# Reordering the stages of a fused decoder block on eight cores: start-up, attention projections, output buffers, and the passage from mixer to MLP

## The chip, the cores and the metric

One Trainium2 chip, eight cores, one program on all of them. Each core handles one half sequence (4096 tokens) of four sequences of 8192, with a halo of earlier tokens that it recomputes. The time is device microseconds (us) of the slowest core. Executions come in two states. In the slow one the cores of a die, or of both, show a lower granted TensorE clock and the time is some per cent longer, whatever the kernel. Engines: PE is TensorE (PEld its weight loads), DVE is VectorE, ACT is ScalarE, POOL is GpSimd, SP is SyncE, which issues the plain transfers; POOL issues the transfers that cast f32 weights to bf16.

## The reference, cut to what matters

```python
h = rms_norm(x, norm_mix_g)
a_b, a_c, a_v, q, k, v, g_a, g_b = split(h @ w_in)          # 1024 -> 5888 columns
y_a = (a_b * causal_dwconv(a_c * a_v)) @ w_proj_a           # gated convolution
# attention: 12 heads of 64 in 3 groups, window/dilation (128,1), (512,4), (2048,16)
y_b = merge_by_denominator(dilated_window_attention(q, k, v)) @ w_proj_b
x = x + (sigmoid(g_a + b0) * y_a + sigmoid(g_b + b1) * y_b) @ w_out
h = rms_norm(x, norm_ffn_g)
gate, val = split(causal_dwconv(h @ w_up))                  # 2 x 2816 columns
x = x + (silu(gate) * val) @ w_down
return rms_norm(x, final_norm_g)
```

## The kernel before

The kernel has three phases. A *tick* is one call of the hook that the program puts between groups of matmuls: it emits the next step of the norm, of a U block or of an attention item. A norms x (written as bf16 to a buffer `h_d` in memory), projects V, K and Q, and runs the attention items; an item is two score matmuls, an exponential on ACT, a mask multiply, and four value matmuls, and every second item sends an unnormalised output U (128 x 264 f32) to memory. B reads h and U back: convolution branch, merging of U, gates, output projection. C is the MLP. All phases share one on-chip arena, so a buffer's place is also an order: a new tenant waits for the old one.

A helper records every operation, with the keys that it reads and writes, and derives the waits. The program is therefore told here by the order of such calls. The start: one semaphore for all small constants, tile -1 (halo) first, and a loop that norms each block from end to end on VectorE.

```python
cdma(flagt_f := sb("flagf", [128, 16], F32), flag_d[:, :], "flagf")
emit_xload(); emit_xload()
wload(wK01, wcols(2304, 512), ("wK01",))
cdma(g1b, g1_d.partition_broadcast(128), ("g1b",))
...                                       # V, K2, V2, masks, Q, Q2, five small constants
for o_ in cops:
    o_.ev = cops[-1].ev                   # every constant waits for the last one
...                                       # memsets of Qz01, Qz2, QhZ on VectorE

def norm_front(...):                      # statistics and multiply in one go
    norm_mul(..., norm_stat(xap, xkey, hbap, hbkey, n))

SEQ = [-1, 0, -2, 1, "E", -3, 2, -4, 3, 4, 5, 6, 7]
for _ in range(10):
    tick(force=True)                      # the first blocks before any matmul
```

The attention items: two in flight, three output buffers, the masks of the third group all on POOL.

```python
LAG = 2
def mask_eng(st):
    return "pool" if st["g"] == 2 else "dve"
...
    if c == 1:
        ui = un[0] % 3                    # UA: 3 output buffers
        copy(pick(430, 400), UA[ui], ps[b][:, 0:4 * VW], ...)
        S.add("sp", lambda e: e.dma_start(out=dst, in_=UA[ui]), ...)
```

The end of A: the third group's V2, K2 and Q2 of tiles 4 to 7 in a pass of their own that reads h back, then the strided V, then B's weights and the last 32 items.

```python
        if t < 4:
            ...                           # V2, K2, Q2 of tiles 0..3 inside the tile
hs_load(0); hs_load(1)                    # tiles 4..7 of h from h_d
...
for jj in range(4):
    ...                                   # v_2, k_2, q_2 on hS
while att or att2 or pend:
    att_tick()
v2_load(2)
wload(wPB, ...); wload(wPA, ...); wload(wO, ...)
push_g2(2)                                # the last 32 items
hb_load(0)
while att or att2 or pend:
    att_tick()
...
for _ in range(3):
    ub_load()                             # only now the first U blocks
```

The passage from B to C: everything of the second norm after B's last output projection.

```python
        else:                             # last tile of B
            for p in (6, 7, 8, 9, 10):
                wu_load(p)                # ten half weights, issued by POOL
            wout(j)
for p in range(3):
    wd_load(p)
...
xn_load(); xn_load()
for _ in range(1 + len(BB[0])):
    c_stat(); c_mul(); c_back()
```

The softmax here doesn't subtract the row's maximum and nothing guards it: scores larger than these inputs give would overflow.

Of the kernel before, what the change touches and what calls it, by code (L numbers as in the profile page):

```python
# [128 lines left out]
def build_program():  # L129
# [129 lines left out]
    def cdma(dst, src, key):  # L259
        cops.append(S.add("sp", lambda e: e.dma_start(out=dst, in_=src), writes=[key], dma_sem=sem_c))  # L260
# [8 lines left out]
    hTA = [buf("hTA%d" % i, (W + 43520 + i * 8192) if i < 2 else R1 + 16384, [128, KC, 512], BF16) for i in range(3)]  # L269
# [8 lines left out]
    UA = [buf("UA%d" % i, R3 + 41344 + i * 1056, [128, 4 * VW], F32) for i in range(3)]  # L278
    V1s = [buf("V1s_%d" % i, R5 + i * 2112, [128, 4, 4, VW], BF16) for i in range(3)]
    K2 = [buf("K2_%d" % i, R4 + i * 8192, [128, 2, 16, 128], BF16) for i in range(2)]  # L280
    Qz2 = buf("Qz2", R4 + 16384, [128, 2, 16, 2, 128], BF16)
    V2 = [buf("V2_%d" % i, W + 8192 + i * 8448, [128, 16, 4, VW], BF16) for i in range(2)]
# [8 lines left out]
    sem_ht = [newsem("s_ht%d" % i) for i in range(3)]  # L291
# [4 lines left out]
    sem_u = [newsem("s_u%d" % i) for i in range(3)]  # L296
# [30 lines left out]
    SEQ = [-1, 0, -2, 1, "E", -3, 2, -4, 3, 4, 5, 6, 7]  # L327
# [3 lines left out]
    for t in SEQ:  # L331
        if t == "E":
            continue
        s_ = k % 3
        k += 1
        slot_of[t] = s_
        prev_in_slot[t] = last.get(s_)
        last[s_] = t
# [23 lines left out]
    cdma(flagt_f := sb("flagf", [128, 16], F32), flag_d[:, :], "flagf")  # L362
# [3 lines left out]
    cdma(g1b, g1_d.partition_broadcast(128), ("g1b",))  # L366
    gdma(ident, cmat_d[:, 0:128], "ident")
    emit_xload()
    emit_xload()
    wload(wV01, wcols(3072, 512), ("wV01",))  # L370
    wload(wK2, wcols(2816, 256), ("wK2",))
    wload(wV2, wcols(3584, 256), ("wV2",))
    gdma(mask4, cmat_d[:, 128:640], "mask4")
    gdma(hmask, cmat_d[:, 640:704], "hmask")
    wload(wQ01, wcols(1536, 512), ("wQ01",))
    wload(wQ2, wcols(2048, 256), ("wQ2",))
    cdma(bg, bg_d[:, :], "bg")
    cdma(caw, caw_d[:, :], "caw")
    cdma(cab, cab_d[:, :], "cab")
    cdma(fcw, fcw_d[:, :], "fcw")  # L380
    cdma(fcb, fcb_d[:, :], "fcb")
    for o_ in cops:
        o_.ev = cops[-1].ev
    for o_ in gops:
        o_.ev = gops[-1].ev
    S.add("dve", lambda e: e.tensor_copy(out=flagt, in_=flagt_f), reads=["flagf"], writes=["flagt"])
    S.add("dve", lambda e: e.memset(onest, 1.0), writes=["onest"])
    scale_g(g1b, ("g1b",))
    for i in range(2):
        S.add("dve", lambda e, i=i: e.memset(Qz01[i].rearrange("p a b c d -> p (a b c d)"), 0.0),  # L390
              writes=[("Qz01_%d" % i, c, h) for c in range(4) for h in range(2)])
    S.add("dve", lambda e: e.memset(Qz2.rearrange("p a b c d -> p (a b c d)"), 0.0),
          writes=[("Qz2", c, jj, h) for c in range(2) for jj in range(4) for h in range(2)])
    S.add("dve", lambda e: e.memset(QhZ.rearrange("p a b c -> p (a b c)"), 0.0), writes=["QhZ"])
# [32 lines left out]
    nf, nt = [0], [0]  # L427
    front_tick = {}
    tickno = [0]

    def can_front(i):
        t, b = NBL[i]
        return t == "E" or prev_in_slot[t] is None or prev_in_slot[t] in done_tiles

    def front(i):
        t, b = NBL[i]
        n = 16 if t == "E" else 128
        norm_front(xA[i % 4], ("xA%d" % (i % 4),), hbA[i % 2], ("hbA%d" % (i % 2),), n, g1b, ("g1b",))
        emit_xload()
        front_tick[i] = tickno[0]  # L440
# [17 lines left out]
    def norm_tick(force=False):  # L458
        if nt[0] < nf[0] and (force or tickno[0] - front_tick[nt[0]] >= 2):
            back(nt[0])  # L460
            nt[0] += 1
        if nf[0] < len(NBL) and nf[0] - nt[0] < 2 and can_front(nf[0]):
            front(nf[0])
            nf[0] += 1
# [10 lines left out]
    LAG = 2  # L475

    def mask_eng(st):
        return "pool" if st["g"] == 2 else "dve"

    def stage_a(st):  # L480
        k_ = att_n[0]
        att_n[0] += 1
        sbk = 4 + k_ % 2
# [15 lines left out]

    ob = [0]  # L500
    un = [0]

    def stage_b(st):
# [12 lines left out]
        if c == 1:  # L516
            ui = un[0] % 3
# [74 lines left out]
    def push_g2(s):  # L592
        cur, prv = s % 2, (s + 1) % 2
        rows = u_d[4 + 2048 * (s - 1):4 + 2048 * s, 2, :].rearrange("(i r) c -> r i c", r=16)
        for r in range(16):
            for c in range(2):
# [6 lines left out]
                                ck=[("K2", cur, s), ("K2", prv, s - 1), ("Q2", 0, s)],  # L603
# [1034 lines left out]
```

## Time and profile before

| | |
|---|---|
| median of the first 3 executions | 2384.74 us (2379.39 to 2619.54) |
| TensorE busy, profiled core (2393.8 us) | 85% |
| first B convolution, mean of 8 cores | 682.7 us |
| from there to the first up-projection | 739.3 us |
| from there to the end | 947.8 us |

B's first convolution and C's first up-projection are both the first matmuls with 388 columns after a gap, because the first tile of both phases is 388 wide. These three stages, as means over the cores of one fast profiled execution, add up to the mean span. The lines of the profile that carry the argument stand in the prediction. One more of before is from the table of waits in B from 735 to 1379.5 us, without its first 35 us (engine, line and tile that waited, for whom; us in total, times, longest us), where L1058 is the transposition of a normalised U block and L1044 the multiply that makes it:

```profile
PE ps L1058 <- DVE arena L1044: 17.2, 19, 1.8
```

TensorE meets 19 U blocks whose multiply is not done yet, for about 0.9 us each. In B's first 35 us (700 to 735) there are four more such waits, 12.0 us.

### The profile page before, as it was taken

What the parts mean: (1) busy time and instruction counts of PE and PEld (TensorE: products, weight loads), DVE (VectorE), ACT (ScalarE), POOL (GpSimd) and SP (SyncE); (2) the same over time, 40 slices, a digit from 0 to 9 for tenths busy, and PEclk for the clock granted to TensorE, in tenths of its full rate; (3) what the DMA queues carried; (4) which work ended last, traced back from release to release, by engine and by line L of the source; (5) the groups of instructions that cost most, each with busy time, mean ns of one, the idle gap of its engine ahead of it and who ended that gap; (6) DMA issues with size and microseconds to landing.
All of it is one profiled execution on the core that took longest, in us unless ns stands there. A gap on an engine that the chain in (4) does not pass through costs nothing.

```text
span 2393.8 us, 38186 instructions; the slowest of 8 cores (2354.9 to 2393.8 us)
## 1 busy us (share of the span) xinstructions
PE 2043.7 (85%) x11550; PEld 1049.2 (44%) x11550; DVE 1270.1 (53%) x2171; ACT 856.3 (36%) x1791; POOL 622.3 (26%) x1216
## 2 busy tenths in 40 slices
PE   0578767794658999999999928999999999999998
PEld 0344444452425555444444414555554444444443
DVE  4455554551224444443443316677677676858583
ACT  1243334441322222212111205455455453636362
POOL 1000000230141211111001223454454444434342
PEclk9999889997859999999999968999999999999999
DMA  9544356239651623330221597201201112111101
GB/s 154 113 111 99 100 117 146 62 80 174 123 138 62 129 87 98 98 115 25 92 95 36 88 164 145 80 26 65 71 28 62 63 45 71 45 72 36 62 19 44
DMA packets 128319, 205.88 MB, mean 86 GB/s; under 512 B 9684, under 2 KB 90330, under 8 KB 127736
## 3 DMA queue, kind: packets, MB, share of 16 engines
q1 hardware_dynamic: 86072, 169.19, 24.9%
q0 software_dynamic: 42048, 34.26, 10.7%
q8 instruction: 98, 1.61, 0.3%
q14 instruction: 101, 0.83, 0.1%
HBM read 177.05 MB, written 60.63 MB: 99 GB/s over the span
## 4 chain that ended last, share of the span: by engine, by line
PE 68%; DVE 10%; issue 9%; DMA 7%; POOL 3%; ACT 2%; SPq 1%; DVEq 1%; POOLq 0%; ACTq 0%
PE ps L608 47%; PE ps L1409 12%; PE ps L614 3%; PE ps L1204 3%; DMA u_d<-arena 3%; DMA arena<-h_d 2%; DVE arena L1358 2%; PE ps L420 2%; DVE arena L409 1%; DVE rtmp L319 1%; POOL arena L495 1%; PE ps L488 1%; DMA fcb_s<-fcb 1%; DVE rstd L321 1%; PE ps L512 1%
## 5 line engine op out<-in xcount | busy, mean ns | idle before, releaser
L608 PE MATMUL ps<-arena 128*128 128x512 bf16 (+5 forms) x6848 | 1352.3, 359 | 2.7 <-DVE arena L424 2.0
L608 PEld LDWEIGHTS ps<-arena 128*128 128x128 bf16 x6848 | 664.2, 98 | 655.9 <-issue 19.2
L1358 DVE SCALAR_TENSOR_TENSOR arena<-ps,fcw_s,arena 128x511 f32<-128x511 f32 (+4 forms) x792 | 524.9, 687 | 108.2 <-ACT uc L1349 30.3
L1409 PE MATMUL ps<-arena 128*128 128x512 bf16 x1408 | 311.3, 379 | 5.0 <-POOL arena L1362 2.8
L1351 ACT ACTIVATE arena<-ps,fcb_s,fcw_s 128x512 f32<-128x512 f32 (+1 forms) x396 | 284.3, 730 | 0.0
L401 ACT ACTIVATE arena<-arena 128x1024 bf16<-128x1024 f32 (+1 forms) x114 | 120.0, 1053 | 351.9 <-DVE arena L1415 205.1
L1371 POOL TENSOR_TENSOR arena<-arena 128x512 bf16<-128x512 bf16 (+1 forms) x198 | 210.5, 1063 | 97.9 <-ACT uc L1349 60.4
L1172 DVE TENSOR_TENSOR arena<-ps,arena 128x512 f32<-128x512 f32 (+2 forms) x144 | 91.0, 633 | 251.7 <-PE ps L608 245.6
L1409 PEld LDWEIGHTS ps<-arena 128*128 128x128 bf16 x1408 | 136.2, 98 | 167.3 <-issue 10.3
L420 PE MATMUL ps<-ident,arena 128*128 128x128 bf16 (+2 forms) x656 | 58.0, 240 | 152.5 <-DVE arena L409 147.5
L1158 ACT ACTIVATE arena<-ps,bg_s 128x512 f32<-128x512 f32 (+2 forms) x144 | 92.1, 640 | 252.4 <-PE ps L608 252.4
L252 ACT ACTIVATE arena<-ps 128x512 bf16<-128x512 f32 (+4 forms) x152 | 82.7, 544 | 219.9 <-PE ps L608 126.5
L1369 ACT ACTIVATE arena<-arena 128x512 bf16<-128x512 f32 (+1 forms) x198 | 115.2, 582 | 114.6 <-POOL arena L1362 97.6
L614 PE MATMUL ps<-arena 128*128 128x256 bf16 (+2 forms) x688 | 125.6, 340 | 35.8 <-DMA arena<-h_d 34.5
L491 ACT ACTIVATE arena<-ps 128x512 bf16<-128x512 f32 x192 | 109.7, 595 | 123.2 <-PE ps L488 62.9
L1175 POOL TENSOR_TENSOR arena<-arena 128x512 bf16<-128x512 f32 (+2 forms) x72 | 82.6, 1148 | 264.0 <-DVE arena L1172 238.0
L495 POOL TENSOR_TENSOR arena<-arena,mask 128x512 bf16<-128x512 bf16 x64 | 72.0, 1151 | 284.2 <-ACT arena L491 284.1
L512 PE MATMUL ps<-arena 128*128 128x66 bf16 x768 | 60.0, 206 | 97.7 <-DVE arena L495 48.9
L1362 POOL TENSOR_TENSOR arena<-arena,corr 128x2 f32<-128x2 f32 x352 | 84.2, 242 | 203.2 <-DVE arena L1358 192.3
L409 DVE SCALAR_TENSOR_TENSOR arena<-arena,rstd 128x1024 bf16<-128x1024 f32 (+1 forms) x82 | 105.3, 1285 | 58.7 <-POOL rstd L321 51.3
L420 PEld LDWEIGHTS ps<-ident,arena 128*128 128x128 bf16 (+2 forms) x656 | 47.9, 109 | 174.8 <-issue 165.4
L1204 PE MATMUL ps<-arena 128*128 128x512 bf16 (+1 forms) x528 | 120.2, 383 | 2.5 <-POOL arena L1175 2.5
(88 smaller groups left out, 1223.5 us busy)
## 6 DMA issues: line engine op xcount, KB each, us to landing
arena<-x_loc SPq DMA_DIRECT2D x80, 512.0 KB, 4.8
arena<-x_d SPq DMA_DIRECT2D x64, 512.0 KB, 3.6
x_d<-arena SPq DMA_DIRECT2D x32, 512.0 KB, 4.0
out<-arena SPq DMA_DIRECT2D x32, 512.0 KB, 2.6
u_d<-arena SPq DMA_DIRECT2D x96, 132.0 KB, 3.5
arena<-u_d SPq DMA_DIRECT2D x32, 396.0 KB, 3.3
arena<-w_up POOLq DMA_DIRECT2D x22, 512.0 KB, 18.5
arena<-w_in POOLq DMA_DIRECT2D x10, 1024.0 KB, 28.0
```

Of the source, the lines that this page charges most:

```text
L401: S.add("act", lambda e: e.activation(out=junk[0:n, :], in_=xap[0:n, :], func=AF.Square, accum_out=ssq[0:n, col:col + 1]), reads=[xkey] + ...
L409: S.add("dve", lambda e: e.scalar_tensor_tensor(out=hbap[0:n, :], in0=xap[0:n, :], scalar=rstd[0:n, col:col + 1], in1=gb[0:n, :], op0=ALU. ...
L420: S.add("pe", lambda e, kc=kc: e.transpose(out=psb[t][:, kc * 128:kc * 128 + n], in_=hbap[0:n, kc * 128:(kc + 1) * 128], identity=ident[0: ...
L491: S.add("act", lambda e: e.activation(out=PA[pi], in_=ps[sbk], func=AF.Exp, scale=0.125), reads=[("ps", sbk)], writes=[("PA%d" % pi,)])
L608: S.add("pe", lambda e, kc=kc: e.matmul(out, lhsT=wap[:, kc, col0:col0 + 128], rhs=rhs(kc), start=(kc == 0), stop=(kc == kcn - 1), skip_gr ...
L614: S.add("pe", lambda e, kc=kc: e.matmul(out, lhsT=lhs(kc), rhs=wap[:, kc, c0:c0 + n], start=(kc == 0), stop=(kc == KC - 1), skip_group_che ...
L1204: S.add("pe", lambda e, b=b, kc=kc, hf=hf: e.matmul(ps[b][0:n, :], lhsT=mT[:, kc, c0:c0 + n], rhs=wO[:, kc, hf * 512:(hf + 1) * 512], star ...
L1351: S.add("act", lambda e, b=b, t=t, ch=ch, w2_=w2_: e.activation(out=tmpC[t][:, 0:n], in_=ps[b][:, o:w_], func=AF.Identity, scale=w2_, bias ...
L1358: S.add("dve", lambda e, b=b, t=t, sh=sh, wv_=wv_, lo=lo: e.scalar_tensor_tensor(out=tmpC[t][:, lo:n], in0=ps[b][:, o + lo - sh:w_ - sh], ...
L1369: S.add("act", lambda e: e.activation(out=actT[:, p, 0:n], in_=tmpC[tg][:, 0:n], func=AF.Silu), reads=[("tmpC%d" % tg,)], writes=[("actT", ...
L1371: S.add("pool", lambda e: e.tensor_tensor(out=actT[:, p, 0:n], in0=actT[:, p, 0:n], in1=tmpC[tv][:, 0:n], op=ALU.mult), reads=[("tmpC%d" % ...
L1409: S.add("pe", lambda e, b=banks[hf], k_=k_, kk=kk, wt=wt, hf=hf: e.matmul(ps[b], lhsT=actT[:, k_, bi * 128:(bi + 1) * 128], rhs=wt[:, kk, ...
```

## The change

Its intent: keep TensorE fed where it idles. (1) x and V's weight first, tile 0 before tile -1, own semaphores, norm split into three steps that overlap. (2) Four h buffers on chip, V2, K2 and Q2 inside every tile, no reload. (3) Seven output buffers, four items in flight, half of the third group's masks and (from block 8 on) the small norm operations moved between engines. (4) B's first U blocks before the last items have ended, and U blocks paced. (5) C's first norm under B's last tile. Also in the diff: six on-chip banks for scores in place of two for the last 32 items (the *drain* of A, below), memsets moved from VectorE to ScalarE and POOL, and the convolution and gate weights loaded before A's projections have ended. Cut to its core:

```diff
-    SEQ = [-1, 0, -2, 1, "E", -3, 2, -4, 3, 4, 5, 6, 7]
+    SEQ = [0, -1, -2, 1, "E", -3, 2, -4, 3, 4, 5, 6, 7]
-    cdma(flagt_f := sb("flagf", [128, 16], F32), flag_d[:, :], "flagf")
+    emit_xload()
+    cdma(g1b, g1_d.partition_broadcast(128), ("g1b",), newsem("s_g1b"))
+    emit_xload()
+    wload(ident, cmat_d[:, 0:128], "ident")
+    wload(wV01, wcols(3072, 512), ("wV01",))
 ...
+        cols_a[i] = norm_stat(xA[i % 4], ..., n, "dve" if i < 8 else "pool")
 ...                                     # stat, mul and back are separate steps of a tick
-    LAG = 2
+    LAG = 4
-        return "pool" if st["g"] == 2 else "dve"
+        return "pool" if st["g"] == 2 and st["r"] % 2 else "dve"
-            ui = un[0] % 3
+            ui = un[0] % 7
 ...
-        if t < 4:
+        (V2, K2, Q2 in every tile)
-    hs_load(0)
-    hs_load(1)
-    (pass over tiles 4..7)
 ...
     hb_load(0)
-    while att or att2 or pend:
-        att_tick()
     for _ in range(3):
         ub_load()
+    while att or att2 or pend:
+        att_tick()
+        if ub_f[0] < 2 and len(att2) < 16 - 8 * ub_f[0]:
+            ub_front()
+    hb_load(1)
+    wload(wO, ...)
 ...
-        if (… ub_f[0] - ub_b[0] < 2 and ub_list[ub_f[0]][0] - 2 <= b_done[0]):
+        if (… and (force or ub_list[i][0] == 0 or tickno[0] - max(ub_ltick[i], ub_tick.get(i - 1, 0)) >= 6)):
             ub_front()
 ...
         if j == 8:
             for p in (3, 4, 5):
                 wu_load(p)
+            begin_c()                    # x1, gain row, statistics and multiply of two blocks
 ...
         else:
+            mid_c()                      # their transposes, and two more blocks
             for p in (6, 7, 8, 9, 10):
                 wu_load(p)
             wout(j)
-    for p in range(3):
-        wd_load(p)                       # now at pairs 4, 8 and 12 of C's first tile (a pair: 128 gate and 128 value columns)
```

## The prediction

> **What bounds the kernel now.** I read the page first: busy shares, slices, then the chain that ended last.
>
> ```profile
> PE 2043.7 (85%) x11550; PEld 1049.2 (44%) x11550; DVE 1270.1 (53%) x2171; ACT 856.3 (36%) x1791; POOL 622.3 (26%) x1216
> ...
> PE   0578767794658999999999928999999999999998
> ...
> PEclk9999889997859999999999968999999999999999
> DMA  9544356239651623330221597201201112111101
> ```
>
> TensorE is busy 85% of the span and no other engine comes near, so I look for its idle time: 2393.8 - 2043.7 = 350 us. A slice is 59.8 us. The idle lies in the first 13 slices (0 to 778 us, one of them full) and in the 24th; the rest is 90% or nearly so. I then cut the span where the program changes stage and asked for busy time and clock in each stretch (start:end, length, busy PE, PEld, DVE, ACT, POOL with counts, granted clock, DMA share, GB/s).
>
> ```profile
> 0.00:98.00 98.00, 16.70 (x118) 11.71 (x119) 49.39 (x100) 16.94 (x29) 9.80 (x31) 1.00 0.82 142
> 98.00:155.00 57.00, 49.56 (x380) 28.57 (x379) 22.44 (x52) 20.77 (x38) 0.59 (x3) 1.00 0.45 103
> 155.00:540.00 385.00, 297.65 (x2176) 168.46 (x2176) 209.04 (x486) 162.57 (x314) 38.31 (x35) 0.91 0.46 102
> 540.00:700.00 160.00, 81.78 (x577) 46.43 (x576) 30.08 (x61) 40.82 (x72) 42.60 (x42) 0.70 0.75 138
> 700.00:735.00 35.00, 22.99 (x129) 12.75 (x130) 17.76 (x45) 3.77 (x7) 0.39 (x2) 0.75 0.61 177
> 735.00:1379.50 644.50, 624.82 (x3275) 311.86 (x3273) 270.13 (x468) 136.96 (x211) 99.84 (x119) 1.00 0.31 82
> 1379.50:1395.50 16.00, 15.66 (x64) 6.56 (x64) 5.06 (x8) 0.00 (x0) 5.89 (x7) 0.89 0.95 147
> 1395.50:1446.60 51.10, 3.38 (x32) 2.64 (x33) 7.85 (x9) 5.54 (x9) 13.71 (x30) 0.55 1.13 182
> ```
>
> Idle: 81 us before the first full tile at 98, 95 in 98:540 (attention, "phase A"), 78 in 540:700, 12 in 700:735, 48 in 1395:1446 (the passage from the mixer, B, to the MLP, C). That is 314 of the 350; B and C are TensorE-bound and stay. What each waits for, from the chain in order of time (start, us, what):
>
> ```profile
> 6.70 18.60 DMA fcb_s<-fcb
> ...
> 402.75 12.36 DMA u_d<-arena
> ...
> 457.41 13.36 DMA u_d<-arena
> ...
> 548.41 46.29 DMA arena<-h_d
> ...
> 635.03 15.41 DMA arena<-v_d
> 652.37 23.90 DMA u_d<-arena
> ...
> 709.89 11.29 DMA arena<-u_d
> ```
>
> The start waits for the last small constant (one shared semaphore), then for 16 us of memsets on VectorE and eight norm blocks in series at 5.07 us each. The waits of 12, 13 and 24 us are score outputs that cannot leave their three buffers. The 46 us is tiles 4 to 7 of h read back from memory, the 15 us the strided V that has just been written. In 98:540 the table of waits puts most of TensorE's idle at a score mask on VectorE (48.1 us, 23 times) and the norm multiply (20.7 us).
>
> **What the Trainium skill says.** "TensorE: Matmul & The Clock Gate", Part 1, gives N/2.4 GHz + 2.5 ns start to start warm, half the rate after an idle window. The trace agrees: eight 512-column matmuls take 1.73 us (0.216 each) in the busy stretches, and the granted clock falls to 0.70 and 0.55 in the idle ones. So removed idle also speeds the work beside it. "DMA: Bandwidth & Descriptors", "Issuing engines are not separate DMA queues", says that transfers of all engines interleave on the same 16 engines. The trace agrees: in the first 60 us the casting weight loads (4.90 MB, 64.3%) and the plain loads (4.31 MB, 29.0%) together fill 93%. The weights move 4.90 / (0.643 x 60) = 127 GB/s of what they write, the plain loads 248. "GPSIMD Engine Reference", section 3.1, has two-input elementwise work slower there than on VectorE; here a mask takes 1151 ns on POOL against 456 ns on VectorE.
>
> **The change, part by part.** I need A's TensorE work at the warm rate, from counts in the source. 1112 matmuls of 512 columns x 0.216 = 240 us; 408 of 256 columns x 0.109 = 44; 192 attention items x 0.34 (0.22 score + 0.12 value, start to start at 502.8) = 65; 45 blocks of transposes x 0.44 = 20; halo and small ones about 14 (estimate from their busy times). Sum 384 us, against 446 busy us spread over 700.
>
> (a) Start. x block 0 is issued first, each constant has its own semaphore, V's weight leads, tile 0 goes ahead of tile -1, and the norm is split so that statistics, multiply and transpose of different blocks overlap. x 0 should land at 7 us (x loads took 5.5 us from issue in the first 60); the gain row is the later input: the view of DMA issues gives it 11.5 us, so 13 plus 1.06 to scale. VectorE then needs about 4.2 us a block (six small operations 1.9, multiply 1.28, copy 0.69, and gaps) so tile 0 is ready at about 31 us. The six weights (4.90 MB, 39 us) share the DMA engines with some 4 MB of x (16 us) and land by 55. Tile 0 has 35 us of TensorE work: 31 + 35 + some waiting for weights = 70 us. In the kernel before 49.6 us of such work was done only at 155.
>
> (b) The rest of A. V2, K2 and Q2 of tiles 4 to 7 are computed while h is on chip (four h buffers), so the 46 us reload is gone and the V round trip lies under tile 7's projections. Seven output buffers instead of three cover 14 items, more than the 13 us stores. Four items in flight instead of two cover the mask's queueing, and 37 of 45 blocks' small norm operations (1.9 us each, 70 us) leave VectorE for POOL. Remaining work: 384 - 35 (tile 0) - 2 (its transposes) = 347, of which the last 32 attention items (11 us) run alone. For the other 336 I take 90% TensorE efficiency: the kernel before reached 79% in 98:540 with the waits named above, 92.5% in 500:540 where few occur, and B has 97%. 336 / 0.90 = 373 us.
>
> (c) The last 32 items. Before they ran at 1.1 us each, POOL's mask time back to back. Now half of the masks are VectorE's: POOL 16 x 1.15 = 18 us, ScalarE 32 x 0.6 = 19 plus copies, TensorE 0.65 an item at the cold clock = 21. I take 25 us.
>
> End of A: 70 + 373 + 25 = 468 us, against 700: 232 us less.
>
> (d) B. The first U blocks are now loaded and normalised during the 32 items, and B's weights and h before; of the 35 us in 700:735 some 18 go. The pacing of the U blocks should save half of the 17.2 us that B's transposes wait for them, 8. From B's first matmul to the last gate it took 679.5 us; predicted 653.
>
> (e) Passage to C. The 51 us of reloading x1, scaling, and norming four blocks moves under B's last tile and its output projection; the projection (16 us) then meets the first up-projection. Given back: the ten half weight loads at 1379 kept POOL issuing until 1412.6 us (ring waits of 10.7 and 14.8 us), so the gate products wait until 33 us after the last gate, with C's first group now starting at 16. Seven temporaries and eight banks hold about six pairs of 2.6 us; VectorE at 4 x 0.61 a pair cannot catch up quickly. And 11 MB of weights at about 120 GB/s end 92 us after the last gate, while the down-projection wants the last part at about 86. I charge 10. From the last gate to the end: 1014.3 - 51 + 10 = 973 us.
>
> Sum: 468 + 653 + 973 = 2094 us on the slowest core of a profiled run; the timed median is 10 us below the profiled one, other cores may differ, and I have counted no surprise. I predict 2100 us, 12% less.
>
> **Rivals.** First, A becomes bound by DMA. It moved some 83 MB and had busy share x time of about 390 us in 700 us; with the reload gone some 375 remain for 468 us, 80%. Bursts would then delay x or output stores: the weights for B (8 MB written) now land in tiles 5 to 7. For it: the saturated slices of the DMA row; against it: the share is 0.46 in 155:540. If it holds, A runs at 75 to 80%: +50 to 70 us, 2150 to 2170. Second, a chain of small operations takes over: POOL's six norm operations plus mask, or VectorE's queue, stall TensorE in order. VectorE had 209 us in 385 and will be near 55%; POOL some 37 x 2.5 + 18 us in 370. I think this costs under 20 us. Third, the gain was hidden anyway: the idle of A returns as B waiting for weights or U. Against it, B's weights are issued tens of us earlier than they are used; for it, POOL's issue waits. That would make 2130. Fourth, TensorE at over 95% throughout draws a lower clock; B and C ran 600 us at 98% with clock 1.00, so I give it little.
>
> **Range and chances.** A at 95% and a clean passage give 2100 - 19 - 15 = 2065, a little more from the start 2055. The first two rivals together give 2170. So 2055 to 2170. To end within 2% the change would have to lose 250 of 290 us, from places that are separate: faster 0.97, within 2% 0.02, slower 0.01.
>
> **What would show it.** First full-width matmuls at about 31 us and the end of tile 0 at about 70; no h_d in any load before the mixer's own; A ending at 455 to 500 with TensorE at 88% or more and a clock near 1; no output-store wait over 5 us in the chain; B's start without its 11 us wait; 16 us, not 67, between last gate and first up-projection, then some 10 us of waits on POOL's gate product or the down weight. Wrong would be: a DMA share near 1 all through A with TensorE at 75%, or a gap at B's start.

## The result, and the profile after

The kernel after took 2141.76 us in the median (2137.3 to 2316.21, 12 executions, one slow), the kernel before 2386.43 on the same chip. A ratio here is the mean time of one kernel's fast executions over the mean of the other's fast executions of the same rounds, so not quite the ratio of the medians. It is 0.8988, with a 95% interval of 0.8969 to 0.9007: 10.1% less. From the page of the profiled execution (busy time of the engines; then slices of 53.5 us):

```profile
PE 1990.2 (93%) x11391; PEld 1036.7 (48%) x11550; DVE 1231.0 (58%) x1973; ACT 865.1 (40%) x1798; POOL 669.4 (31%) x1408
...
PE   3889989968999999999999979999999999999998
...
DMA  9665867596362233032037951201111102020201
```

TensorE is now 93% busy. (159 of this core's 11550 matmul records are missing from the trace, x11391 beside x11550 weight loads; core 7, with all of them, is busy 1999.7 us, so the busy figures below are slightly low.) Three dips are left: the first slice, the ninth and tenth (a 6 and an 8, 428 to 535 us) and the 24th (a 7). The stretches of the same core (start:end, length, busy PE, PEld, DVE, ACT, POOL with counts, granted clock, DMA share, GB/s), cut at the stage boundaries, show how much they cost:

```profile
0.00:28.20 28.20, 4.07 (x33) 3.15 (x34) 20.46 (x42) 16.03 (x16) 9.82 (x23) 1.00 0.96 216
28.20:80.30 52.10, 38.93 (x190) 18.93 (x194) 16.38 (x33) 13.78 (x24) 2.93 (x10) 0.87 1.01 145
80.30:444.80 364.50, 337.44 (x2724) 205.72 (x2764) 207.77 (x355) 195.78 (x374) 109.49 (x274) 1.00 0.68 148
...
452.50:494.90 42.40, 18.82 (x198) 12.27 (x195) 19.40 (x40) 17.95 (x32) 20.57 (x19) 0.70 0.79 178
494.90:1159.70 664.80, 641.86 (x3355) 323.89 (x3398) 290.31 (x517) 143.63 (x222) 101.48 (x121) 0.99 0.35 93
...
1180.50:1240.00 59.50, 58.11 (x353) 34.46 (x354) 45.29 (x77) 38.28 (x103) 25.12 (x34) 1.00 1.12 199
1240.00:1262.30 22.30, 8.57 (x25) 3.11 (x25) 7.63 (x14) 4.94 (x14) 3.66 (x4) 0.69 0.78 142
```

Tile 0 begins at 28.2 and ends at 80.3 us. From there to 444.8, where the ordinary tiles of A lie, TensorE is busy 337.44 of 364.50 us, 92.6%, at full clock and a DMA share of 0.68. The last 32 items, the drain of A, take 42.40 us with 18.82 of work, at a clock of 0.70. The two last rows are C's first tile: up-projections without a gap, then 22 us with 8.6 of work. Note the DMA column (it adds up the time of all packets as a share of 16 engines, and so can exceed 1): about 1 at the start, 0.79 in the drain of the items, 1.12 just before that last gap. Each of the dips is a stretch of crowded DMA. The table of waits of the whole execution, and one row of POOL's own between 1150 and 1260 us, name what was waited for:

```profile
PE ps L544 <- DVE arena L254: 21.0, 8, 13.2
PE ps L1088 <- DVE arena L1074: 20.6, 14, 2.4
...
PE ps L1465 <- DMA arena<-w_dn: 13.7, 2, 9.8
...
PE ps L641 <- DMA arena<-w_in: 10.5, 1, 10.5
```

```profile
POOL arena L1143 <- issue: 24.5, 2, 16.0
```

L544 is the value matmul, L254 the copy of its result into an output buffer on VectorE. The copy is named because it came last. What VectorE itself waited for from 430 to 500 us is in its own table of waits, where L1067 is the first step of normalising a U block:

```profile
DVE zt L1067 <- DMA arena<-u_d: 11.3, 1, 11.3
...
DVE arena L254 <- DMA u_d<-arena: 4.0, 2, 2.6
```

The change itself put this U step among the last items. Its block, issued at 455.6, had not landed, and from 465.4 to 476.7 VectorE stood at it with the next mask and copy behind it. That is most of the 13.2 us, and it is so on all eight cores: 9.3 to 14.2 us for U, 0 to 4.0 us for output buffers. In before (640 to 735 us) VectorE stood 24.5 us for buffers. The chain of waits (start, us, what) shows stores all the same:

```profile
452.17 8.66 DMA u_d<-arena
...
464.40 17.23 DMA u_d<-arena
...
1223.24 35.41 DMA arena<-w_dn
```

A store took 17 us, and after the U step the copy at 481.7 waited 2.6 us more for its buffer; that last wait is what the chain follows. How long the items would have waited for buffers without the U step, all else equal, no run shows. L1088 is the transposition of a U block (L1058 of before): 20.6 us in all of B against 17.2 + 12.0 before; without B's first 35 us it is 16.2 against 17.2. The third wait is the down-projection's weight, whose chain piece starts at 1223, where POOL issued it; POOL itself had stood 24.5 us in the issue of earlier weights. The fourth is Q's weight at 56 us.

The three stages, means over the cores of a profiled execution:

| | A: to B's first convolution | B: to the first up-projection | C: to the end | mean span |
|---|---|---|---|---|
| before | 682.7 | 739.3 | 947.8 | 2369.8 |
| after | 487.3 | 686.1 | 960.4 | 2133.8 |
| difference | -195.4 | -53.2 | +12.6 | -236.0 |

The gain comes from A (83% of it) and from the passage, which is counted in B; C gives 12.6 us back. On the core that ended last, A ended at 494.87, the latest of the eight (482.0 to 494.9), so a part of what that one core shows is chance.

### The profile page after: what moved, and what is told of

The parts are those of the page before. It is cut to its first block, busy times and chain, and to the rows that moved or that the text cites. A ratio compares the mean times of both kernels' runs of the same rounds, so it can differ in the third digit from the quotient of the medians.

```text
span 2140.3 us, 37892 instructions; the slowest of 8 cores (2126.0 to 2140.3 us)
## 1 busy us (share of the span) xinstructions
PE 1990.2 (93%) x11391; PEld 1036.7 (48%) x11550; DVE 1231.0 (58%) x1973; ACT 865.1 (40%) x1798; POOL 669.4 (31%) x1408
## 4 chain that ended last, share of the span: by engine, by line
PE 80%; DMA 5%; DVE 5%; issue 4%; ACT 2%; POOL 2%; another core or an unknown queue 0%; SPq 0%; DVEq 0%; POOLq 0%; ACTq 0%
PE ps L641 54%; PE ps L1465 13%; PE ps L1244 5%; PE ps L647 3%; DMA arena<-w_dn 2%; DMA arena<-x_loc 1%; DVE arena L1414 1%; PE ps L519 1%; PE ps L423 1%; DMA u_d<-arena 1%; DVE arena L412 1%; PE ps L544 1%; DVE arena L1074 1%; PE ps L1088 1%; ACT arena L404 1%
## 5 line engine op out<-in xcount | busy, mean ns | idle before, releaser
L641 PE MATMUL ps<-arena 128*128 128x512 bf16 (+4 forms) x6748 | 1340.5, 357 | 22.9 <-DMA arena<-w_in 10.5
L1465 PE MATMUL ps<-arena 128*128 128x512 bf16 x1372 | 310.2, 382 | 19.5 <-DMA arena<-w_dn 13.7
L316 POOL TENSOR_SCALAR ssq<-ssq 128x1 f32<-128x1 f32 (+1 forms) x102 | 24.0, 235 | 364.2 <-ACT arena L404 313.9
L1471 DVE TENSOR_TENSOR arena<-ps,arena 128x512 f32<-128x512 f32 x64 | 44.1, 690 | 146.8 <-PE ps L1465 146.8
L526 DVE TENSOR_TENSOR arena<-arena,mask 128x512 bf16<-128x512 bf16 x160 | 74.3, 472 | 79.2 <-ACT arena L522 77.4
L647 PE MATMUL ps<-arena 128*128 128x256 bf16 (+2 forms) x676 | 115.7, 318 | 4.2 <-DVE arena L427 3.5
L1405 ACT ACTIVATE uc<-ps 128x2 f32<-128x2 f32 x396 | 66.3, 167 | 116.7 <-PE ps L641 115.3
```

The lines of the kernel that those rows point to most:

```text
L641: S.add("pe", lambda e, kc=kc: e.matmul(out, lhsT=wap[:, kc, col0:col0 + 128], rhs=rhs(kc), start=(kc == 0), stop=(kc == kcn - 1), skip_gr ...
L647: S.add("pe", lambda e, kc=kc: e.matmul(out, lhsT=lhs(kc), rhs=wap[:, kc, c0:c0 + n], start=(kc == 0), stop=(kc == KC - 1), skip_group_che ...
L1465: S.add("pe", lambda e, b=banks[hf], k_=k_, kk=kk, wt=wt, hf=hf: e.matmul(ps[b], lhsT=actT[:, k_, bi * 128:(bi + 1) * 128], rhs=wt[:, kk, ...
```

## The experiments

Twelve kernels ran, all correct. They ran on chips 8, 11 and 12, each batch beside the kernel before. The means of the kernel before's fast executions differ between the batches by up to 0.4% (2382.2, 2376.9, 2376.7, 2373.0, 2376.8), the changed kernel's perhaps not by the same amount. A difference from after can be taken from the ratios (against 0.8988, times 2376) or from the means of fast executions (against 2141.1); the two disagree by 4 to 8 us. Both are given, and a difference under 10 us settles nothing by itself. The stage columns are the surest: means over eight cores of one execution, after's 487.3, 686.1 and 960.4. Their scatter can be read where a stage is the same program: A is 487.3, 484.5 and 488.0 in after, c_late and c_early; B is 684.3 to 686.4 and C 959.6 to 960.4 in after and the five kernels that change A alone (reload, ua3, lag2, start_old, dve_norm).

| kernel | ratio to before, 95% | against after, us (by ratio / by means) | A | B | C |
|---|---|---|---|---|---|
| reload | 0.9098, 0.9068 to 0.9129 | +26 / +22 | 505.9 | 684.3 | 960.1 |
| c_late | 0.9125, 0.9084 to 0.9166 | +33 / +28 | 484.5 | 730.8 | 944.0 |
| ua3 | 0.9096, 0.9061 to 0.9131 | +26 / +21 | 506.3 | 686.4 | 959.9 |
| lag2 | 0.9084, 0.9057 to 0.9112 | +23 / +18 | 508.4 | 685.0 | 959.8 |
| start_old | 0.9091, 0.9061 to 0.9120 | +24 / +18 | 504.3 | 685.0 | 959.6 |
| dve_norm | 0.9015, 0.8986 to 0.9044 | +6 / +1 | 489.6 | 685.7 | 959.8 |
| x_gate | 0.9037, 0.9013 to 0.9061 | +12 / +7 | 495.9 | 683.8 | 958.8 |
| c_early | 0.8934, 0.8909 to 0.8959 | -13 / -18 | 488.0 | 684.8 | 943.6 |
| w_late | 0.9021, 0.9001 to 0.9040 | +8 / 0 | 473.0 | 698.8 | 959.8 |
| loads_late | none given (2 of 4 slow) | - / -2 | 490.4 | 683.5 | 957.2 |
| x_gate2_ublag | 0.8886, 0.8866 to 0.8906 | -24 / -32 | 480.8 | 662.3 | 958.5 |
| best | 0.8799, 0.8775 to 0.8823 | -45 / -51 | 472.1 | 663.7 | 943.0 |

The theory: the gain is the sum of separate idle pieces that each part of the change removes, and what is missing to the predicted 2100 us lies where transfers crowd (start, drain of the items, C's first tile) and in B's transposes. The first five kernels each undo one part. The main rival to each is that its piece would have been hidden anyway, as TensorE fills the time with something else.

**reload.** V2, K2 and Q2 of tiles 4 to 7 go back to a pass that reads h from memory.

```diff
+        if t >= 4:
+            done_tiles.add(t)
+            return
 ...
+    hs_load(0)
+    hs_load(1)
+    while att2:
+        tick(force=True)
+        att_tick()
+    for jj in range(4):
+        (v_2, k_2, q_2 from the reloaded h, as in before)
```

(The full edit also keeps partly covered arena buffers on record and changes the pace of the attention items after tile 3.)

> The changed kernel with one part undone: V2, K2 and Q2 of tiles 4 to 7 are again computed in a pass of their own, from h read back from memory. Theory (idle time taken out of TensorE's path): the same matmuls, but the read back of h, the round trip of V2 just before it is needed, and attention with less projection work to hide behind return; 40 to 70 us more, so about 2195 us, with a wait of 15 to 45 us on the h read in the chain. Rival (phase A is bound by the bytes that the DMA engines move): only 4 MB more of about 80 are moved, so 10 to 20 us more, about 2155 us.

Measured: ratio 0.9098, A longer by 18.6 us, B and C as in after. The waits of TensorE, and the chain:

```profile
PE ps L645 <- DMA arena<-h_d: 19.6, 1, 19.6
```

```profile
403.79 21.36 DMA arena<-h_d
```

One wait of 19.6 us for h, where before had 34.5 us in two. The form is the theory's (a wait for h of 15 to 45 us), the size is the rival's by the A column (10 to 20) and below the theory's 40 to 70 by every column. The rival's reason is not excluded: during the wait (403.8 to 425.2 us) the DMA share is 1.08, as a casting weight of 1 MB was in flight beside the two h reads.

**c_late.** The passage of before: the second norm, the down weights and all loads for C after B's last output projection.

```diff
-            begin_c()
-            mid_c()
-            if j == 0 and p in (4, 8, 12):
-                wd_load(p // 4 - 1)
+    for p in range(3):
+        wd_load(p)
+    begin_c_late()                        # loads, gain row, four blocks in series on POOL and VectorE
```

> The changed kernel with the passage from mixer to MLP undone: the first norm blocks of the MLP are prepared only after the mixer's last output projection, and the down weights are issued there. Theory: TensorE's idle of 51 us comes back and the 13.7 us wait for the down weight goes; 33 to 42 us more, about 2180 us. Rival (most of this gain was given back to the weight loads): under 20 us more.

Measured: 0.9125; two of four executions were slow. The theory held, at the low edge of its 33 to 42 us by the ratio. The stages show what the total hides: B with the passage is 44.7 us longer and C 16.4 us shorter. TensorE's wait for the first norm multiply is back (45.6 us of this row lie between 1100 and 1260):

```profile
PE ps L423 <- DVE arena L412: 58.5, 14, 29.1
```

So the passage is worth 45 us and costs 16 elsewhere: with the old passage the down weights have landed by the time that they are wanted.

**ua3.** Three output buffers instead of seven.

```diff
-            ui = un[0] % 7
+            ui = un[0] % 3
```

> The changed kernel with three output buffers for attention in place of seven. Theory of the prediction (stores of 12 to 24 us stall TensorE when there are only three buffers): 25 to 45 us more, about 2175 us, with several waits over 5 us on the output store before tile 7. Rival (the stalls at the end of A come from the DMA engines whatever the buffers, and elsewhere stores are fast): under 10 us more, about 2148 us.

Measured: 0.9096, A longer by 19.0: just under the theory's 25 us, and over its low edge by the ratio only.

```profile
PE ps L545 <- DVE arena L254: 36.9, 13, 12.8
```

```profile
349.82 20.88 DMA u_d<-arena
...
474.02 16.64 DMA u_d<-arena
```

A store of 17 us at the end of A is there with three buffers and with seven. What changes is who stands for it: over A, VectorE and ScalarE waited 52.2 us for output buffers with three (30.8 of them from 80 to 440 us) and 4.0 with seven. Less of it reached TensorE than the theory named: before 440 us it waited for such copies only twice, 4.3 and 4.0 us, not several times over 5. So the extra buffers do cover the stores, in the ordinary tiles and in the drain.

**lag2.** Two items in flight instead of four.

```diff
-    LAG = 4
+    LAG = 2
```

> The changed kernel with two attention items in flight in place of four. Theory of the prediction (four cover the queueing of the mask on VectorE): TensorE's waits for the mask come back; 15 to 30 us more, about 2165 us. Rival (it is the norm's small operations, which have left VectorE, that made the mask late before): under 6 us more, about 2145 us.

Measured: 0.9084, A longer by 21.1 us. The theory held: the value matmul now waits for the mask, on POOL and on VectorE, 33 times (14.1 us of it from 80 to 440, the rest later).

```profile
PE ps L544 <- POOL arena L526: 18.4, 17, 3.3
...
PE ps L544 <- DVE arena L526: 15.0, 16, 6.7
```

**start_old.** The order of loads, the shared constant semaphore, the memsets on VectorE and the tile order of before; the split norm stays.

```diff
-    SEQ = [0, -1, -2, 1, ...]
+    SEQ = [-1, 0, -2, 1, ...]
-    emit_xload()
-    cdma(g1b, g1_d.partition_broadcast(128), ("g1b",), newsem("s_g1b"))
-    (ident, V's weight first)
+    (flag, x, K's weight, gain row on the shared semaphore, ..., five constants, then memsets)
```

> The changed kernel with the start undone: tile -1 first, the constants on one semaphore and in the old order, K's weight first, all memsets on VectorE ahead of the first norm. Theory of the prediction (the end of tile 0 moved from 155 to about 80 us; some of this is the norm's pipelining and the order of tiles, which the second part of the undoing leaves in place): first full matmuls at 50 to 60 us in place of 28, 25 to 45 us more in all, about 2175 us. Rival (the DMA engines are full until the last weight lands whatever the order, so a late start catches up): under 10 us more, about 2150 us.

Measured: 0.9091, just under what the theory named; A longer by 17.0 us.

```profile
PE ps L432 <- DVE ssq L316: 54.1, 5, 45.2
```

TensorE first works at 45 us instead of 13, and its first projections begin at 58 instead of 28, a loss of 30; yet A ends only 17 us later. When the late start is over all weights have landed, and the wait for Q's weight is gone. So about half of what the new start gains is given back at once, and the visible part of that is the wait for weights.

**dve_norm.** All small norm operations on VectorE, as in before.

```diff
-        ... n, "dve" if i < 8 else "pool")
+        ... n, "dve")
```

> The changed kernel with the small norm operations of phase A all on VectorE, as before (37 blocks x 1.9 us = 70 us of its time). Theory of the prediction (they delayed masks and evacuations on VectorE): 10 to 25 us more, about 2160 us, with TensorE's waits for the norm multiply and for masks up from 10 and 1 us. Rival (with four items in flight VectorE's queue is covered): under 5 us more, about 2145 us.

Measured: 0.9015, A longer by 2.3 us, which is inside the scatter. The interval overlaps after's; the rival held. Over the ordinary tiles VectorE is 247 us busy instead of 208 and POOL 28 instead of 109, with TensorE the same to within a microsecond. VectorE had the room. What had left it was thus 40 us of busy time; the 70 us of the prediction counted the gaps between the six operations too.

**x_gate.** The fifth x block waits for Q's weight, so that the weights go first.

```diff
+              reads=[("wQ01",)] if i == 4 else [], writes=[("xA%d" % sl,)], dma_sem=sem_x[sl])
```

> The changed kernel where the loads of x from the fifth block on wait until Q's weight has landed. Theory (x loads that are not needed yet and stores, 4.1 MB, take the DMA engines from the weights, and make the 10.5 us wait for Q's weight): Q's weight lands at 40 to 46 us, that wait goes, tile 0 ends at 70 to 74 us in place of 80; if tile -1 does not wait for x in turn, 4 to 10 us less in all, about 2135 us. Rival (what the weights gain the x blocks lose): the wait moves to the norm of tile -1, and the total stays within 3 us.

Measured: 0.9037, slower, A 8.6 us longer: neither the theory's 4 to 10 us less nor the rival's 3 us. The fifth x block was issued by 36 us, so Q's weight had landed by then and not at 56; its wait is gone (K and Q run straight through, 13.98 us of matmuls in a row), but another is twice as long:

```profile
PE ps L647 <- DVE arena L427: 21.4, 1, 21.4
```

L427 is the copy of block 3's transposed norm, and it belongs to tile 0. VectorE had been given block 4's statistics ahead of block 3's copy, and block 4's x was now late: block 3's transposes were done at 24.6 us, but VectorE stood 20.0 us, until 43.4, for block 4's sum of squares from ScalarE, which itself stood 17.4 us for x, and copied block 3 only at 45.2. The edit delayed its own tile. A transfer can be moved back only together with the operations that wait for it.

**c_early.** Three of C's up weights earlier, so that POOL's queue is free sooner and the down weights find less traffic.

```diff
-            for p in (3, 4, 5):
+            for p in (3, 4, 5, 10):        # at the start of B's last tile
 ...
+            if j == 8 and oc == 3:
+                wu_load(6)
+                wu_load(7)
-            for p in (6, 7, 8, 9, 10):
+            for p in (8, 9):
```

> The changed kernel where three of the MLP's up weights are issued earlier: one at the start of the mixer's last tile, two after its fourth gate, when the gate weights beneath them are free. Theory (the down weight is late because 11 MB of weights are asked for only at the last gate and the DMA engines are full until it lands): the 13.7 us wait for the down weight falls under 3 us, POOL's issue waits after the last gate shrink, total 8 to 14 us less, about 2131 us. Rival (the down weight is late because it is issued late, at the 5th, 9th and 13th pair): the wait stays over 8 us and the total within 4 us.

Measured: 0.8934, faster; C is 16.8 us shorter and so even under before's 947.8, A and B as in after. The wait for the down weight has left the table, and POOL's issue waits between 1100 and 1260 fell from 25.1 to 6.9 us. The theory held: c_late's 16 us and these 17 are the same cost, and it is one of transfers, not of the overlapped norm.

**w_late and loads_late.** The drain, from both sides. When these runs were planned, the wait of 13 us was taken for a store wait. It could then come from the two casting weight loads issued just before the last 32 items (w_late issues them after), or from the loads of h and U blocks on the same queue as the stores (loads_late issues those after).

```diff
 w_late
-    wload(wPB, ...)
-    wload(wPA, ...)
 ...                                       # the last 32 items
     hb_load(1)
+    wload(wPB, ...)
+    wload(wPA, ...)
     wload(wO, ...)

 loads_late
-    hb_load(0)
-    for _ in range(3):
-        ub_load()
 ...                                       # the last 32 items, and in their loop:
-        if ub_f[0] < 2 and len(att2) < 16 - 8 * ub_f[0]:
-            ub_front()
+    hb_load(0)
+    for _ in range(3):
+        ub_load()
     hb_load(1)
```

> The changed kernel where the two branch projections' weights (2.6 MB) are issued after the last 32 attention items, not before them. Theory (those loads take the DMA engines from the output stores, and TensorE waits 13 us for a store although there are seven buffers): the longest wait on an output buffer in the drain falls under 4 us and the drain from 42 to about 28 us; B then waits for the weights at its first gate, 5 to 15 us; total within 8 us of the changed kernel. Rival (the stores queue behind the plain loads of h and U that are issued ahead of them on the same queue): the wait stays at 10 us or more and the total rises 5 to 20 us.

> The changed kernel where the loads of h and of the first three U blocks for B (2 MB, on the queue of the output stores) are issued after the last 32 attention items, not before them; the weights stay before. Theory of the rival above (the stores queue behind these loads): the longest wait on an output buffer falls under 4 us, the drain takes about 28 us, and B's start waits 10 to 25 us for h and U. Theory of the weights: the wait stays at 8 us or more, and B's wait comes on top; total 10 to 25 us more.

Measured: w_late 0.9021 and, by means, the very time of after; of loads_late two executions were slow, the fast ones are 2138.34 and 2139.24 us. In w_late TensorE's waits for output copies fell from 21.0 to 9.5 us and A ended 14.3 us sooner, but B is 12.7 us longer. The table of waits from 430 to 520, then TensorE in order of time with the idle before a group in brackets, then the chain:

```profile
PE ps L544 <- DVE arena L254: 9.5, 6, 4.0
```

```profile
523.19 0.80 PE L1086 MATMUL ps<-ident,arena 128*128 128x128 bf16 x6 [14.30 <-DVE arena L1072]
```

```profile
488.98 32.18 DMA arena<-u_d
```

B began at 478 us on this core, ran for 31 us, and stood 14.3 us for a U block that took 32 us to land, issued after the weights, h and four x blocks; the expectation had been a wait for the weights. In loads_late the waits for output copies also shrank, to 7.0 us, and B then waited for h:

```profile
PE ps L641 <- DMA arena<-h_d: 23.3, 1, 23.3
...
PE ps L544 <- DVE arena L254: 7.0, 10, 1.6
```

In both runs the first U block no longer stops VectorE among the items. In w_late it has landed in time, and in the drain VectorE waits neither for U nor for a buffer; the two longest waits left, 3.5 and 4.0 us, are the U steps themselves between two copies. In loads_late the U steps come after the items, and VectorE waits 6.6 us for buffers in seven pieces. The items take 31 and 28 us on these cores and not 42. But the total is unchanged in both, against 10 to 25 us more expected of loads_late: around the end of A the engines have to move a given amount before B can run, and either order pays it once: as a U wait among the items, as a U wait in B or as an h wait. The way out is to take something out of that window that nobody needs yet.

**x_gate2_ublag.** Two repairs at once, in places that do not meet: x_gate with the norm steps of block 4 and later also held back until tile 0's four blocks are transposed, and U blocks transposed four ticks after their multiply instead of two.

```diff
+              reads=[("wQ01",)] if i == 4 else [], ...
-        if ns[0] < len(NBL) and ns[0] - nm[0] < 2 and (force or ncred[0] >= 1):
+        if ... and (ns[0] < 4 or tickno[0] - stamp.get("four", tickno[0]) >= 7):
-        if ub_b[0] < ub_f[0] and (force or tickno[0] - ub_tick[ub_b[0]] >= 2):
+        if ub_b[0] < ub_f[0] and (force or tickno[0] - ub_tick[ub_b[0]] >= 4):
```

> Two edits in stages that do not meet. Start: x loads from the fifth block on wait for Q's weight as in the earlier run, but the norm of these blocks is also emitted later, so that neither VectorE's nor TensorE's queue meets them before V and K of tile 0 are done. Theory (the earlier run lost its gain because block 3's copy stood behind block 4's statistics on VectorE): first full matmuls at 24 to 26 us, no wait over 4 us for V's, K's or Q's weight, tile 0 ends at 60 to 70 us, tile -1 without a wait over 5 us; 8 to 18 us less. Rival (DMA bytes set the start in any order): tile 0 may end earlier but tile -1 or -2 waits for x, and the same tile order is reached within 4 us of the changed kernel. B: the transposes of a U block are emitted four ticks after its multiply, not two. Theory (they wait because VectorE meets the multiply late, behind an evacuation): their waits fall from 20 us to under 8, and B's length by 8 to 14 us. Rival (the waits come from the pacing, at each group's end): under 4 us.

Measured: 0.8886; two of six executions were slow. A is 6.5 us shorter (8 to 18 expected) and B 23.8 (8 to 14 expected), so the two can be told apart by stage. The whole of B has this one wait for U left:

```profile
PE ps L1090 <- DVE arena L1076: 0.6, 1, 0.6
```

The wait was a matter of distance in the program. Two ticks are too near for VectorE's queue; the pacing that came with the change spaced the multiplies but left the transposes where they were. At the start full-width matmuls begin at 25.6 us and the wait for Q's weight is gone (1.1 us is left for a weight of the third group), but tile 0 ends at 75 us and not at 60 to 70. A new wait of 6.1 us for ScalarE's copies takes back half. It is x_gate's fault again, on another engine: ScalarE had been given the next block's statistics and stood for its x.

```profile
69.81 1.06 ACT L404 ACTIVATE arena<-arena 128x1024 bf16<-128x1024 f32 x1 [10.47 <-DMA arena<-x_loc]
```

**best.** c_early and x_gate2_ublag together, with a lighter drain: B's two projection weights after the last items, and the output weight, the second h and four x blocks (nothing needs them for some 60 us) only after the second of eight output groups of B's first tile.

```diff
     (wPB, wPA as in w_late)
-    hb_load(1)
-    wload(wO, ...)
-    for _ in range(4):
-        xb_load()
 ...
             gate_oc(j, oc)
+            if j == 0 and oc == 1:
+                wload(wO, ...)
+                hb_load(1)
+                for _ in range(4):
+                    xb_load()
```

> The early up weights of c_early, the gated x blocks with the four-tick lag of x_gate2_ublag, and a new order of transfers around the end of phase A: the two projection weights of B are issued after the last 32 items (as in w_late), and the output weight, the second h and the four x blocks, about 7 MB read, only after the second of the eight output groups of B's first tile, since the output projection wants them first some 60 us after that. Theory (what counts at the end of A is the sum of what is read before B can run; w_late began B at 478 us but then stood 14.3 us for a block of U behind the weights): store waits at the end of A below 10 us in sum, B's first convolution at about 466 (478 less the 12 that x_gate2_ublag gained earlier), no wait over 4 us in B's first tile, and all three gains add: 0.0054 + 0.0102 + some 0.005 under 0.8988, a ratio near 0.878, about 2087 us. Rival 1: the transfers are only moved once more, and the output projection of the first tile then waits 10 us or more for its weight or x: ratio 0.882 to 0.884, about 2098. Rival 2: the gains overlap, and the ratio stays at 0.888.

Measured: 2090.49 us (2087.24 to 2375.42, six executions, one slow), ratio 0.8799 with 0.8775 to 0.8823. The theory's 0.878 is inside the interval, and so is the lower edge of the first rival's range. Waits of TensorE from 420 to 620 us, and the stretch of B on the profiled core:

```profile
PE ps L546 <- DVE arena L254: 9.2, 7, 3.4
...
PE ps L1244 <- DMA arena<-w_out: 4.2, 1, 4.2
```

```profile
475.90:1124.30 648.40, 642.05 (x3398) 324.40 (x3398) 289.50 (x517) 143.65 (x222) 106.71 (x129) 0.99 0.41 102
```

B now runs at 99% from its first matmul, and A's end of w_late (473.0) is kept (472.1) without the price in B; in the drain VectorE waits neither for U nor for a buffer. Of the rival, 4.2 us is left: the output weight came a little late. What failed is the date of B's start, 475.9 on this core against 466 expected: I had added x_gate2_ublag's gain in A to w_late's, and the stages show that they overlap (-6.5 and -14.3 make -15.2 together). Against after, A, B and C are shorter by 15, 22 and 17 us.

## Why the prediction was right or wrong

The verdict (faster) and the range were right; the centre was 42 us low. On the profiled slowest core the sum was 2094 and the span 2140.3, and the 46 us split by the prediction's own terms into 27 for A's end, 12 for B and 8 for the last stage. No error of one of these three cancelled another's, but this core's A ended 7.6 us after the mean of the eight.

**Start: first projections right, tile 0 mis-sized.** Full-width matmuls began at 28.2 us (31 predicted; the gain row landed in 5.9 us and not 11.5). Tile 0 ended at 80.3, not 70. The step that failed is "the six weights ... share the DMA engines with some 4 MB of x (16 us) and land by 55". By 56 us the casting queue had moved 3.87 MB (as written) and the plain one 7.01 MB: ten x loads of 0.5 MB, a gain row and a store of h were issued before, and Q's weight landed 10.5 us late on this core (2 to 10 on all). That it is the traffic is shown by x_gate, where Q's weight landed by 36 us and the casting queue had moved 4.90 MB by 56. The full repair is worth 6.5 us in A by x_gate2_ublag, since a wait for x takes its place.

**A's ordinary tiles: right, with some luck.** 373 us were predicted; from the end of tile 0 to the last 32 items (80.3 to 452.5) it took 372.2. 90% was assumed, 92.6% measured to 444.8, with the clock at 1.00, but the work had been counted as 336 us and TensorE was busy 342.4: two errors of some 2% cancel. The first rival (A bound by DMA, TensorE at 75 to 80%) was wrong for these tiles, at a DMA share of 0.68, but right for the start and the drain. The second rival's chain of small operations cost little: dve_norm says 2 us. What left VectorE was no part of the gain beyond that.

**The last 32 items: mis-sized by an overlap that failed.** 25 us predicted, 42.4 measured. The step that failed is "The first U blocks are now loaded and normalised during the 32 items", taken together with a count of the engines' work only: the first U block had not landed, and VectorE stood 11.3 us for it with the items' masks and copies behind. In loads_late, where the U steps come after the items, these take 28 us, near the 25. The term "Seven output buffers instead of three cover 14 items, more than the 13 us stores" held by effect, since VectorE waited 4.0 us for buffers, but its 13 us was the wrong figure: the prediction's own lines show a store of 23.9 us in this window of before, and one took 17.2 in after, so the sign "no output-store wait over 5 us in the chain" failed. w_late and loads_late show that mere reordering returns the time to B; best shows that taking transfers out of the window keeps it. What no run separates is the U step from its load: the step moved behind the items with all loads left in place was not tried.

**B: the term for the pacing was wrong in kind.** 653 predicted, 664.8 measured. "The pacing of the U blocks should save half of the 17.2 us": it saved 1 (17.2 became 16.2, without B's first 35 us). In B's first us, where 18 were to go, about 13 went (an estimate: the first 88 convolution matmuls end 35.7 us after B's start before and 21.5 after, with one us of difference in transposes). The lag from multiply to transposition decides, as x_gate2_ublag shows with 0.6 us.

**Passage: mechanism right, size slightly off.** The first up-projection came 20.8 us after the last gate (16 predicted). The time given back was charged at 10 us, to POOL's issue and the down weight; the waits for the down weight were 13.7 (none for POOL's gate product), stage C lost 12.6 against before, and c_late and c_early put the cost at 16 to 17. B's start no longer waited 11 us for a U load, as predicted.

**The third rival** (A's idle returns as B waiting) did not happen in the change as it is, but w_late shows that it was near. Of the prediction's readings, three are off without changing its argument: a mask takes 432 ns on VectorE in the mean, not 456; busy share times time in A before adds up to 403 us, not about 390; and the 70 us of small operations are 40 us of busy time.

**What stays open.** Undoing one part at a time costs A 18.6 (reload), 19.0 (ua3), 21.1 (lag2), 17.0 (start_old) and 2.3 us (dve_norm), 78 together, of a gain of 195; in B, c_late gives back 44.7 of 53.2. The rest of A is not attributed to parts. That the parts cover each other (an undone part is filled by the others) is a reading that only start_old shows, and the new schedule of items, the mask split and the spreading of V2, K2 and Q2 as an even load were not undone alone. B's earlier U blocks were not separated from the pacing either. By kind rather than by part the two profiled cores do divide it: A is 205 us shorter there, TensorE's idle time in A fell from 254 to 91 us, and its busy time from 446 to 404 for the same weight loads within 7 of 3250 (some us of this are the missing records). So, as an estimate, about a fifth of A's gain is the same matmuls running faster, at granted clocks of 0.91 and 0.70 in 155:540 and 540:700 before and 1.00 in the ordinary tiles after.

## What to carry to other kernels

When idle pieces are separate, their sum is a good prediction, and the errors lie where transfers bunch up at a stage boundary: write down what must land in each such window, and move out what nobody needs yet rather than reorder what is in it. When a wait is put down to an engine's copy, ask what that engine itself stood for. Here it was three times a step that had been given to an engine before its data had landed (the next block's statistics in x_gate and x_gate2_ublag, the first U block in the drain), and other work stood behind: give such a step later, or its transfer earlier. Cut each profile into the same few stages and average over the cores: differences of 7 us that the end-to-end times blur are then plain, and two repairs in one run can be told apart.

## What the Trainium skill lacked or had wrong

- The Trainium skill, "DMA: Bandwidth & Descriptors", section "Queues, rings and completion order", says that an engine takes turns between queues packet by packet (no run here shows the turns themselves). Neither it nor "Issuing engines are not separate DMA queues" says how bytes divide between casting and plain loads. In after's first 56 us the casting queue moved 3.87 MB (as written, in bf16) and the plain one 7.01 MB, each with over half of the engines' time; a casting weight of 1 MB took 30.9 us from issue to landing in the median, a plain 0.5 MB block 8.5.
- No page that I read sizes how much a small store stretches beside such loads. A 132 KB output store took 7.8 us in the median between 430 and 530 us of after, 3.1 us in w_late, and 17.2 us in the chain of after.
- No page that I read says how long POOL itself stands when it issues many weight loads in a row: 25.1 us in three waits in after (1100 to 1260 us), 6.9 us in c_early, where three of the weights were issued earlier.
